# A two-layer encoder trunk on one core: an issue order fixed for the DMA queue, stores moved a few steps, and modulation sums divided differently between two stages

## The chip, the cores and the metric

The kernel runs on one core of a Trainium2 chip. A core has five engines that work side by side, each on its own list of instructions and strictly in that list's order: TensorE (PE, matrix products, with the loading of weights shown apart as PEld), VectorE (DVE), ScalarE (ACT), GpSimd (POOL) and SyncE (SP), which here does nothing but issue transfers (DMAs). They meet through semaphores. The metric is the time of one launch on the device, in microseconds (us); lower is better.

## What is computed

An encoder of two layers over 1024 tokens of width 1024, all in float32. Each layer has an attention half and a feed-forward half, and a vector `c` modulates both:

```
cond = silu(c)
mod = cond @ w_mod[l] + b_mod[l]                    # 1024 -> 6 * 1024
sh_a, sc_a, gt_a, sh_f, sc_f, gt_f = split(mod, 6)
h = rms_norm(x, g_attn) * (1 + sc_a) + sh_a
y = three attention groups over h @ w_in            # A: neighbourhood, B: window, C: dense
x = x + gt_a * (norms(y) @ w_o)
h = rms_norm(x, g_ffn) * (1 + sc_f) + sh_f
gate, up = split(h @ w_gu, 2)                       # 1024 -> 2 * 2816
x = x + gt_f * ((silu(gate) * up) @ w_down)         # 2816 -> 1024
```

A final RMSNorm closes the trunk. The modulation vector of a layer does not depend on the tokens, so its six groups of 1024 columns can be summed at any time before they are used: groups 0 to 2 before and in the attention half, 3 to 5 in the feed-forward half. In what follows "group (1, 2)" is layer 1, third group.

## The kernel before, in words

**Products.** Each float32 operand is split into a high and a low part (ACT casts, DVE or POOL subtracts), and each product is three matmuls. Gate/up and down are done by Strassen's scheme with Winograd's sums: a 2 x 2 block product in seven products instead of eight. In gate/up a step `q` (0 to 21) is one block of 256 columns of the gate matrix (even `q`) or of the up matrix (odd `q`). It has seven products of twelve matmuls; the first five steps have two of their seven done earlier, while the activations are still being normalised. Two steps make a pair, and there are eleven pairs in a layer.

**Gate/up.** `gu_raw` loads the weights of a step (two tiles `wr` of 512 KB), `a_parts` forms sums `ws` on DVE and splits them into tiles `wpt`, and the class `Ahead` keeps eight such parts ready in front of TensorE. `gu_product` runs a product and takes its result out of PSUM: ACT copies it or applies silu, DVE adds, POOL multiplies. The finished pair stands in two tiles `sg`, and the pair after next uses the same two tiles. `g_steps` lists what is left to do with a finished pair: three stores to the DRAM array `gpd` (blocks 11, 22, 21), four subtractions in place on DVE that make the Strassen sums out of the same tiles, and four stores of those sums (t1, t3, t2, t4). After each product `g_step` does one entry of the list, and many entries are empty.

**Down.** `w_first` loads blocks `w` of the down weights (256 KB each), `b_load` reads `gpd` back two units at a time into `graw`. `units()` splits both, and 77 units of twelve matmuls (`ps_d`) follow, the first eleven of which use block 11 of each pair.

**Modulation.** A group is summed over eight row blocks of `w_mod`: a load `wmt`, then on DVE a multiply-add into `acc` (`mod_add`), then `mod_flush`: two parts `acch` and `accl`, matmuls with a matrix of ones (`ps_mod`), and a short reduction. There are two ways in. `mod_next` does one row block of 1024 columns a call (512 KB). It is called after the last projections of the attention input: six times beside the values (`ps_v`) and beside each of the twelve half projections `ps_ab`, there once in layer 0 and three times in layer 1. It loads into four tiles shared with the tables `zt`. `mod_stream` does half a row block a step (512 columns, 256 KB) in gate/up, into the two tiles `sq`, at the products of even index from `q` = 2 on. Layer 0 finishes its own groups there and sums (1, 0) and (1, 1); layer 1 sums the other four beside `ps_ab`.

**What sets the order.** Python emits the instructions, and a scheduler then orders each engine's list by a modelled time. `pin([sp], True)` takes SP out of its hands: SP issues in the order in which Python emitted. It is pinned beside `ps_ab` and in down, and free in gate/up. DVE and ACT are free in all three. A transfer at the head of SP's list that has to wait for a tile holds up all that stand behind it.

Every operation is recorded at line 49 of the kernel (a wrapper around the engines), so the profile is read by tile names.

Of the kernel before, what the change touches and what calls it, by code (L numbers as in the profile page):

```python
# [23 lines left out]
H = 512  # L24
# [61 lines left out]
def trunk(ctx: ExitStack, tc, A, C, out):  # L86
    nc = tc.nc
    pe, act, dve, pool, sp = (
        Engine(tc, e) for e in (nc.tensor, nc.scalar, nc.vector, nc.gpsimd, nc.sync)
    )  # L90

    def pin(engines, on):
        for e in engines:
            e.pinned = on
# [123 lines left out]
    def sub(out, a, b, eng=dve):  # L218
        eng.tensor_tensor(out=out, in0=a, in1=b, op=ALU.subtract)
# [130 lines left out]
    def mod_next(psp, shared, l):  # L350


        if psp is not None:
            mod_flush(psp)
        if not todo or todo[0][0] > l or going["step"] == KC:
            return
        if going["step"] == 0:
            going["acc"] = cp.tile([P, 1024], F32, name="acc", tag="acc")
        mod_step(*todo[0], going["step"], going["acc"], shared)
        going["step"] += 1  # L360
        if going["step"] == KC:
            mod_parts(slice(0, shared[3]), shared)
# [128 lines left out]
    ps_cm, psl = open_pool("ps0", bufs=8, space=PSUM)  # L491
# [200 lines left out]
    for l in range(2):  # L692
# [200 lines left out]
        for t in range(10):  # L893
# [4 lines left out]
            elif t < 6:  # L898
                i = t + 4 if t < 2 else t + 2
# [8 lines left out]
            if 0 < t < 9:  # L908
                t1, t2 = qts.pop(t - 1)
# [26 lines left out]
        ab_cm, ab = open_pool("ab", side="left")  # L936
# [44 lines left out]
        for oc in range(NE, 8):  # L981
            w = wab
            for half in range(2):
                if half == 0 and oc < 7:
                    wab = split_tile(wst.pop(0), KC)
                ps = ab_proj(w, half)
                for _ in range(1 + 2 * l):
                    mod_next(psl, (ab, "zt", 4, 1024), l)
                if store:
                    store()  # L990
                if half == 0 and oc < 6:
                    wst.append(w_ab(l, oc + 2))
                store = ab_split(oc, half, ps, ab)
# [418 lines left out]
        pairs = {}  # L1412
# [3 lines left out]
        for n in range(-AHEAD - 1, N + 1):  # L1416
# [27 lines left out]
            for end, (chunks, width) in norms.items():  # L1444
                if begins[end] <= m <= end and (m - begins[end]) % 8 == 7:
                    i = (m - begins[end]) // 8
                    if end not in gss:
                        gss[end] = gss_tile()
                    for half in range(2):
                        what = lambda a=(chunks, gss[end], i, half): norm_sum(*a)  # L1450
# [25 lines left out]
        ps_cm, psl = open_pool("ps1", bufs=8, space=PSUM)  # L1476
        mp_cm, mp = open_pool("mp", side="left")
        NK = 6
        due = [("row", k) for k in (7, 0, 1)] + [("col", 6), ("col", 7)]
# [64 lines left out]
        nt_cm, ntp = open_pool("nt", side="left")  # L1544
# [85 lines left out]
        def x_tile(n, shape, name):  # L1630
            return xp.tile(shape, F32, name=name, tag=f"x{n}")
# [31 lines left out]
        def gu_product(q, p, a):  # L1663
            num, b, bank = p
            up = q % 2
            t = quads.setdefault(q, {})
            ps = product(num, t, bank, a, hb[b], 4)
            e, o = sg.get(q // 2, (None, None))
            lo, hi = slice(0, H), slice(H, S)

            def take(key, out=None):
                if out is None:
                    tag, bufs = ("u4", 1) if (q, num) == (4, 1) else ("u", 4)
                    out = ffp.tile([P, H], F32, name="u", tag=tag, bufs=bufs)
                t[key] = out
                act.copy(out, ps)

            def add(key):
                dve.tensor_tensor(out=t[key], in0=t[key], in1=ps, op=ALU.add)

            def done(dst, src, eng=dve):
                if up:
                    eng.tensor_tensor(out=dst, in0=dst, in1=src, op=ALU.mult)
                else:
                    act.activation(dst, src, AF.Silu)

            if num == 1:
                take("11")
            elif num == 2:
                add("11")  # L1690
                if e is not None:
                    done(e[:, lo], t["11"], pool)
            elif num == 6:
                take("12", None if up else e[:, hi])
            elif num == 5:
                take("22", None if up else o[:, hi])
            elif num == 7:
                take("x")
                t22 = t["22"]
                pool.tensor_tensor(out=t22, in0=t22, in1=t["x"], op=ALU.add)  # L1700
                done(o[:, hi], t["22"], pool)
            elif num == 3:
                add("12")
                done(e[:, hi], t["12"], pool)
            else:
                done(o[:, lo], ps)
                if up:
                    steps.extend(g_steps(q // 2, e, o))

        steps = []  # L1710

        def g_steps(b, e, o):


            b11, b12, b21, b22 = (t[:, i * H : (i + 1) * H] for t in (e, o) for i in range(2))

            def put(name, src):
                sp.dma_start(gpd[:, PLACE[name] + b, :], src)

            due = {  # L1720
                0: lambda: [put(*a) for a in (("11", b11), ("22", b22), ("21", b21))],
                6: lambda: sub(b11, b12, b11),
                7: lambda: (sub(b12, b22, b12), sub(b22, b22, b11), put("t1", b11)),
                8: lambda: (sub(b21, b21, b22), put("t3", b12), put("t2", b22)),
                9: lambda: put("t4", b21),
            }
            return [due.get(i, lambda: None) for i in range(10)]

        def g_step(n=1):
            for what in steps[:n]:  # L1730
                what()
            del steps[:n]

        def gu_start(b):
            sg[b] = [x_tile(4 + 2 * (b % 2) + i, [P, S], "sg") for i in range(2)]


# [35 lines left out]
            shifted_sub(b21, b21, shift(2 * i + 1), t2)  # L1773
            h_split("t4", i, b21, pool)

        mods_due = mod_stream(psl, (ntp, "sq", 2, H), (1, 2))
        bs = []
        rows = None
        norm = rstd_rows(ssq, ntp, psl)
# [1 line left out]
        for q in range(EARLY):  # L1781
            for i in range(2):
                a = [w[:, 4 * i : 4 * i + 4] for w in early[q]]
# [13 lines left out]
        for part in (t3_part, t4_part):  # L1797
            for q in range(1, 4):
                part(q, *bs[q])
        for q in range(NF):  # L1800
            if q % 2 == 0:
                gu_start(q // 2)
            if q < EARLY:
                up = q % 2
                e = sg[q // 2][0][:, 0:H]
                if up:
                    pool.tensor_tensor(out=e, in0=e, in1=quads[q]["11"], op=ALU.mult)
                else:
                    act.activation(e, quads[q]["11"], AF.Silu)
            for i, p in enumerate(PRODUCTS[2 if q < EARLY else 0 :]):  # L1810
                gu_product(q, p, ahead.get())
                ahead.fill()
                g_step()
                if i % 2 == 0 and q > 1:
                    next(mods_due, None)
        for _ in mods_due:
            pass
# [71 lines left out]
        due = {}  # L1889
# [33 lines left out]
            for i, u in enumerate(us):  # L1923
                at_unit(u, lambda n=n0 + 2 * i, half=half: x_back(n, half))

        pin([sp], True)
        for t in range(NB):
            w_first("11", t, wap)
            if t in (1, 3):
                b_load(t // 2)  # L1930
        ahead = Ahead(units())
        ahead.fill(4)
        g_step(len(steps))
        xt = blocks(xp)
        b_load(2)
        acc_a = [psl.tile([P, 512], F32, name="ps_d", tag="mm") for _ in range(4)]
# [195 lines left out]
```

## Time and profile before

| what | time |
|---|---|
| median of 3 runs | 2643.97 us (2643.47 to 2654.1) |
| the profiled execution | 2648.72 us, its span 2646.6 us |
| granted TensorE clock, mean | 0.967 |
| layer 0: `ps_ab` beside modulation | 193.2 to 263.5 us |
| layer 0: gate/up, down | 641.7 to 1110.7 us, then to 1334.9 us |
| layer 1: `ps_ab` beside modulation | 1479.3 to 1583.8 us |
| layer 1: gate/up, down | 1953.8 to 2402.7 us, then to 2628.0 us |

Rows of the profile name an instruction by output and input tile, with their shapes. In a view of waits, "A <- B: total, times, longest" says how long the instructions of A stood idle until B was done. In a view in order of time, a bracket at the end of a row holds the idle time in front of it and what ended it. In a view by stretches each engine has its busy time and its number of instructions, followed by the granted clock of TensorE, the busy share of the DMA engines and GB/s. "SPq" is SP issuing a transfer; a row of several transfers covers the time from the first to the last issue.

### The profile page before, as it was taken

What the parts mean: (1) busy time and instruction counts of PE and PEld (TensorE: products, weight loads), DVE (VectorE), ACT (ScalarE), POOL (GpSimd) and SP (SyncE); (2) the same over time, 40 slices, a digit from 0 to 9 for tenths busy, and PEclk for the clock granted to TensorE, in tenths of its full rate; (3) what the DMA queues carried; (4) which work ended last, traced back from release to release, by engine and by line L of the source; (5) the groups of instructions that cost most, each with busy time, mean ns of one, the idle gap of its engine ahead of it and who ended that gap; (6) DMA issues with size and microseconds to landing.
All of it is one profiled execution on the core that took longest, in us unless ns stands there. A gap on an engine that the chain in (4) does not pass through costs nothing.

```text
span 2646.6 us, 34697 instructions
## 1 busy us (share of the span) xinstructions
PE 2467.0 (93%) x12071; PEld 2037.8 (77%) x12071; DVE 1809.6 (68%) x2896; ACT 1241.2 (47%) x2335; POOL 964.5 (36%) x881
## 2 busy tenths in 40 slices
PE   5899999899799899899999789998998999998998
PEld 5677899777577788788877668997876888887887
DVE  6845999987965755376747568999677454454865
ACT  5421888934433333344523118888444333333443
POOL 5541445543643343300135104456445444340001
PEclk8999999999999999999999889999998999999999
DMA  8467205074343523396424662050623332327743
GB/s 260 141 186 231 64 21 160 19 247 147 119 142 109 163 81 107 109 278 183 138 82 120 212 209 57 21 155 21 207 80 119 116 104 92 108 84 231 218 140 107
DMA packets 288862, 356.48 MB, mean 135 GB/s; under 512 B 32824, under 2 KB 207120, under 8 KB 288688
## 3 DMA queue, kind: packets, MB, share of 16 engines
q1 hardware_dynamic: 288384, 354.13, 43.5%
q8 instruction: 95, 1.56, 0.2%
q14 instruction: 79, 0.65, 0.1%
q0 software_dynamic: 304, 0.14, 0.0%
HBM read 267.31 MB, written 87.85 MB: 134 GB/s over the span
## 4 chain that ended last, share of the span: by engine, by line
PE 50%; DVE 6%; issue 4%; DMA 2%; ACT 2%; POOL 1%; SPq 1%; POOLq 0%; DVEq 0%; ACTq 0%
PE ps_w L49 21%; PE ps_d L49 13%; PE ps_o L49 3%; PE pv L49 3%; PE ps_ab L49 2%; PE T L49 2%; PE ps_v L49 2%; PE sC L49 1%; DVE xb L49 1%; DVE acc L49 1%; PE ps_st L49 1%; SPq L49 1%; ACT pr L49 0%; DMA cst<-const_rope_dram 0%; PE sA L49 0%
## 5 line engine op out<-in xcount | busy, mean ns | idle before, releaser
L49 PE MATMUL ps_d<-wpt 128*128 128x512 f32 x1848 | 428.2, 393 | 18.0 <-ACT wpt L49 17.7
L49 PEld LDWEIGHTS ps_d<-wpt 128*128 128x128 f32 x1848 | 348.4, 189 | 93.4 <-ACT wpt L49 18.3
L49 POOL TENSOR_SCALAR pr<-pr,rs 128x1024 f32<-128x1024 f32 (+4 forms) x256 | 208.1, 815 | 223.7 <-DVE rs L49 209.4
L49 POOL TENSOR_TENSOR wlo<-wst,whi 128x1024 fp32r<-128x1024 f32 x58 | 146.8, 2534 | 290.0 <-ACT whi L49 281.6
L49 PE MATMUL pv<-pt,vs 128*128 128x256 f32 x1216 | 201.2, 297 | 11.7 <-DVE y L49 5.3
L49 DVE TENSOR_TENSOR pt<-T,pt 128x512 fp32r<-128x512 f32 x304 | 199.7, 681 | 10.2 <-ACT pt L49 8.6
L49 POOL TENSOR_TENSOR wpt<-ws,wpt 128x512 fp32r<-128x512 f32 x88 | 119.5, 1360 | 217.9 <-ACT wpt L49 133.4
L49 PE MATMUL T<-identr,pr 128*128 128x128 f32 x1320 | 192.1, 274 | 5.0 <-POOL pr L49 2.1
L49 ACT CAST pt<-T 128x512 fp32r<-128x512 f32 x304 | 170.1, 587 | 40.3 <-PE T L49 38.4
L49 PEld LDWEIGHTS pv<-pt,vs 128*128 128x128 f32 x1216 | 161.0, 190 | 26.1 <-DVE y L49 12.8
L49 ACT COPY u<-ps_w 128x512 f32<-128x512 f32 x132 | 77.4, 586 | 220.1 <-PE ps_w L49 220.0
L49 PEld LDWEIGHTS T<-identr,pr 128*128 128x128 f32 x1320 | 156.7, 141 | 27.3 <-POOL pr L49 4.4
L49 ACT CAST wpt<-w 128x512 fp32r<-128x512 f32 x154 | 95.5, 620 | 171.6 <-PE ps_d L49 155.5
L49 POOL TENSOR_TENSOR sg<-sg,u 128x512 f32<-128x512 f32 x88 | 124.6, 1416 | 138.2 <-ACT u L49 78.8
L49 DVE TENSOR_TENSOR wpt<-w,wpt 128x512 fp32r<-128x512 f32 x154 | 108.3, 703 | 77.7 <-ACT wpt L49 77.4
L49 DVE TENSOR_TENSOR wpt<-ws,wpt 128x512 fp32r<-128x512 f32 x88 | 78.5, 892 | 102.6 <-ACT wpt L49 102.5
L49 DVE TENSOR_TENSOR ws<-wr 128x512 f32<-128x512 f32 x88 | 86.3, 981 | 90.5 <-POOL wpt L49 81.0
L49 ACT CAST wpt<-ws 128x512 fp32r<-128x512 f32 x176 | 108.2, 622 | 78.7 <-PE ps_w L49 37.6
L49 PE MATMUL ps_w<-ht3h,wpt 128*128 128x512 f32 x352 | 116.6, 414 | 25.7 <-ACT sg L49 24.4
L49 DVE SCALAR_TENSOR_TENSOR acc<-wmt,condT,acc 128x1024 f32<-128x1024 f32 (+1 forms) x85 | 116.6, 1375 | 27.0 <-DMA wmt<-in_w_mod_dram 26.1
L49 ACT CAST whi<-wst 128x1024 fp32r<-128x1024 f32 x74 | 77.0, 1049 | 114.5 <-PE ps_o L49 38.6
L49 DVE TENSOR_TENSOR wpt<-graw,wpt 128x512 fp32r<-128x512 f32 x154 | 108.9, 707 | 28.6 <-ACT wpt L49 28.6
(258 smaller groups left out, 6301.6 us busy)
## 6 DMA issues: line engine op xcount, KB each, us to landing
wr<-in_w_gu_dram SPq DMA_DIRECT2D x92, 512.0 KB, 3.6
gpd<-sg SPq DMA_DIRECT2D x154, 256.0 KB, 2.1
graw<-gpd SPq DMA_DIRECT2D x76, 512.0 KB, 3.8
wmt<-in_w_mod_dram SPq DMA_DIRECT2D x63, 512.0 KB, 5.0
w<-in_w_down_dram SPq DMA_DIRECT2D x110, 256.0 KB, 5.4
qk<-qkd SPq DMA_DIRECT2D x44, 512.0 KB, 7.2
qkd<-qko SPq DMA_DIRECT2D x64, 256.0 KB, 3.9
wst<-in_w_o_dram SPq DMA_DIRECT2D x32, 512.0 KB, 4.5
```

The lines of the kernel that those rows point to most:

```text
L49: ins = op(*args, **kwargs)
```

## The change

1. Layer 1 calls `mod_next` once, not three times, beside each `ps_ab` half.
2. In gate/up `mod_stream` runs to group (1, 4), not (1, 2), and takes a step at every product instead of every second one.
3. The list of a pair has 13 entries, not 10. The first three stores move from entry 0 to 3, the subtractions from 6, 7, 8 to 8, 9, 10, and the stores of the sums to entries 9, 11 and 12.
4. The lists are kept per pair. `gu_start` first finishes every pair but the latest.
5. SP is pinned from the start of the loop over `q`, not from the start of down. The last pair's stores, which the free order had put among the first loads of down, are now emitted behind the first loads of down.

```diff
-                for _ in range(1 + 2 * l):
-                    mod_next(psl, (ab, "zt", 4, 1024), l)
+                mod_next(psl, (ab, "zt", 4, 1024), l)
...
-                    steps.extend(g_steps(q // 2, e, o))
+                    steps.append(g_steps(q // 2, e, o))
...
             due = {
-                0: lambda: [put(*a) for a in (("11", b11), ("22", b22), ("21", b21))],
-                6: lambda: sub(b11, b12, b11),
-                7: lambda: (sub(b12, b22, b12), sub(b22, b22, b11), put("t1", b11)),
-                8: lambda: (sub(b21, b21, b22), put("t3", b12), put("t2", b22)),
-                9: lambda: put("t4", b21),
+                3: lambda: [put(*a) for a in (("11", b11), ("22", b22), ("21", b21))],
+                8: lambda: sub(b11, b12, b11),
+                9: lambda: (sub(b12, b22, b12), sub(b22, b22, b11), put("t1", b11)),
+                10: lambda: sub(b21, b21, b22),
+                11: lambda: (put("t3", b12), put("t2", b22)),
+                12: lambda: put("t4", b21),
             }
-            return [due.get(i, lambda: None) for i in range(10)]
-
-        def g_step(n=1):
-            for what in steps[:n]:
-                what()
-            del steps[:n]
+            return [due.get(i, lambda: None) for i in range(13)]
+
+        def g_step():
+            if steps:
+                steps[0].pop(0)()
+                if not steps[0]:
+                    steps.pop(0)
+
+        def g_finish(pairs):
+
+            while len(steps) > pairs:
+                g_step()
 
         def gu_start(b):
+            g_finish(1)
...
-        mods_due = mod_stream(psl, (ntp, "sq", 2, H), (1, 2))
+        mods_due = mod_stream(psl, (ntp, "sq", 2, H), (1, 4))
...
+        pin([sp], True)
         for q in range(NF):
...
                 g_step()
-                if i % 2 == 0 and q > 1:
+                if q > 1:
                     next(mods_due, None)
...
-        pin([sp], True)
         for t in range(NB):
             w_first("11", t, wap)
...
         ahead.fill(4)
-        g_step(len(steps))
+        g_finish(0)
```

## The prediction, made before the change was run

> **What bounds the kernel now.** I read the page's totals and chain first, then the same stages of the two layers side by side, since the change makes a stage of one layer like that of the other, then the waits inside them.
>
> ```profile
> span 2646.6 us, 34697 instructions
> ...
> PE 50%; DVE 6%; issue 4%; DMA 2%; ACT 2%; POOL 1%; SPq 1%; POOLq 0%; DVEq 0%; ACTq 0%
> ```
>
> The chain runs over TensorE, so time is won only where TensorE stands idle or runs at a low granted clock. The next rows are stretches: `ps_ab` in layers 0 and 1, gate/up in 0 and 1, the first 22 us of down in 0 and 1, and gate/up without modulation. The columns are PE, PEld, DVE, ACT, POOL (busy, instructions), clock, DMA share, GB/s.
>
> ```profile
> 193.20:263.50 70.30, 69.00 (x297) 55.69 (x296) 38.31 (x43) 11.04 (x16) 13.90 (x5) 1.00 0.73 221
> 1479.30:1583.80 104.50, 81.85 (x305) 62.88 (x304) 72.45 (x73) 11.02 (x16) 13.53 (x5) 0.85 0.70 227
> 641.70:1110.70 469.00, 442.40 (x1853) 354.70 (x1853) 284.97 (x350) 170.00 (x298) 200.28 (x140) 0.97 0.34 110
> 1953.80:2402.70 448.90, 435.63 (x1841) 351.07 (x1841) 240.41 (x288) 170.19 (x298) 195.87 (x140) 0.98 0.29 95
> 1110.70:1133.00 22.30, 12.93 (x50) 10.16 (x49) 8.72 (x15) 5.78 (x11) 0.00 (x0) 0.85 1.01 302
> 2402.70:2424.00 21.30, 13.69 (x50) 10.94 (x50) 9.07 (x15) 6.11 (x11) 0.00 (x0) 0.76 1.01 306
> ...
> 1007.00:1048.00 41.00, 41.00 (x178) 33.26 (x177) 19.16 (x24) 15.84 (x28) 16.69 (x13) 1.00 0.29 97
> ```
>
> Three excesses stand out. The same projections take 70.3 us in layer 0 and 104.5 us in layer 1. Gate/up takes 469.0 us in layer 0, which has modulation in it, and 448.9 us in layer 1, which has none. At the start of down TensorE is busy for 13 of 22 us in both layers.
>
> **Step 1: `ps_ab` in layer 1, -34.2 us.** First the waits of TensorE there, layer 1 and then layer 0 (total, times, longest), then the DVE work that reads `wmt` in the two stretches.
>
> ```profile
> PE ps_mod L49 <- DVE acch L49: 22.5, 4, 9.0
> ...
> PE ps_mod L49 <- DVE acch L49: 1.3, 1, 1.3
> ...
> 193.20:263.50 70.30, 22.27 (x17) 1.00 0.73 221
> 1479.30:1583.80 104.50, 45.19 (x32) 0.85 0.70 227
> ```
>
> Layer 1 adds 32 row blocks (45.2 us of DVE) there, and TensorE, which takes `ps_mod` in its own order, stands four times behind the end of a group. The change removes 16 of the 32 loads (8 MB) and adds and two of the four flushes. What is left is, in the instruction order of the changed program, what layer 0 has now: the same DVE list from the first `qko` to the last, less two adds with which layer 0 begins a third group. So 70.3 us replaces 104.5. The gain cannot be much more. At least the idle time goes, 22.5 - 1.3 = 21.2 us; the rest of the 34.2 is matmuls at a granted clock of 0.85, which go back to 1.00 with the idle time. I take 34.2 and keep 21 as the other end.
>
> **Step 2: gate/up of layer 0, -12.5 us.** The 16 blocks come back as 32 half blocks, 66 in all instead of 34, beside products. Matmuls first: layer 0 has 1853 - 1841 = 12 more than layer 1, six flushes of two; the change makes it ten flushes, 20 matmuls. At 41.00 / 178 = 0.23 us that is 4.6 us, so the stage cannot fall below 448.9 + 4.6 = 453.5. Today's other excess is 469.0 - 448.9 - 2.8 = 17.3 us of waits, and this chain shows the largest of them:
>
> ```profile
> PE ps_w L49 <- ACT sg L49: 21.6, 4, 8.1
> ...
> 907.21 0.62 PE L49 MATMUL ps_w<-h11h,wpt 128*128 128x512 f32 x2
> ...
> 917.98 1.64 SPq L49 DMA_DIRECT2D gpd<-sg  x3
> ...
> 921.62 0.69 DVE L49 TENSOR_TENSOR sg<-sg 128x512 f32<-128x512 f32 x1 [1.14 <-DMA gpd<-sg]
> 922.22 0.68 DVE L49 TENSOR_TENSOR u<-u,ps_w 128x512 f32<-128x512 f32 x1
> ...
> 922.94 0.63 ACT L49 ACTIVATE sg<-u 128x512 f32<-128x512 f32 x1 [9.29 <-DVE u L49]
> ...
> 924.10 1.22 PE L49 MATMUL ps_w<-ht3h,wpt 128*128 128x512 f32 x2 [5.58 <-ACT sg L49]
> ```
>
> Read from below: the fifth product of a gate step waits for ACT, ACT for a DVE add, the add stands behind a subtraction in place, and that one waits for the store of the block it overwrites, which SP issued 10.8 us after the step began, behind modulation loads. In steps of 12 x 0.23 = 2.8 us the fifth product is due 11.2 us after the first, and the add started at 15.0 us to make it 5.6 late. So an add up to about 9.4 us after the step's begin costs nothing. In layer 1, without modulation, it comes earlier:
>
> ```profile
> 2129.24 0.62 PE L49 MATMUL ps_w<-h11h,wpt 128*128 128x512 f32 x2
> ...
> 2132.54 1.65 SPq L49 DMA_DIRECT2D gpd<-sg  x3
> ...
> 2136.67 0.68 DVE L49 TENSOR_TENSOR u<-u,ps_w 128x512 f32<-128x512 f32 x1
> ...
> wr<-in_w_gu_dram SPq DMA_DIRECT2D x92, 512.0 KB, 3.6
> gpd<-sg SPq DMA_DIRECT2D x154, 256.0 KB, 2.1
> ```
>
> With SP pinned and the stores at entry 3, SP issues both `wr` loads of a step (1 MB) and then the three stores; the modulation loads come one a product instead of in bursts. The first `wr` lands 3.6 us after its issue; at the 300 GB/s that the start of down shows, the second needs 1.7 us more and the three stores 0.9 each, so the last store lands near 8 us, and the add starts near 8.7: inside 9.4, by little. Hence I leave 3 us of the 17.3: 453.5 + 3 = 456.5, -12.5. Queued behind SP's waits are only loads due seven products (19 us) later, since `Ahead` and the second raw tile cover them. DVE has room: 19.16 of 41 us without modulation. The extra adds cost this:
>
> ```profile
> L49 DVE SCALAR_TENSOR_TENSOR acc<-wmt,condT,acc x14: 739/750/1840, 881.3 to 911.2; 128x512 f32<-128x512 f32 x14
> ...
> DMA wmt<-in_w_mod_dram: 12.1, 8
> ```
>
> At 0.75 us, 32 of them are 24 us over some 13 steps (250 us, one step of `mod_stream` a product); at 1.84 us, 59 us; and the group shown made DVE wait 12.1 us for its loads. All of it fits into DVE's idle time, but each late microsecond in front of that add counts. Bounds: 453.5 (-15.5), and every group paying double, 453.5 + 2 x 17.3 = 488 (+19).
>
> [...]
>
> **Step 3: the start of down, -12.4 us.**
>
> ```profile
> 1109.09 1.30 SPq L49 DMA_DIRECT2D w<-in_w_down_dram  x2
> ...
> 1112.28 0.68 DVE L49 TENSOR_TENSOR sg<-sg,ps_w 128x512 f32<-128x512 f32 x1
> ...
> 1118.45 12.77 PE L49 MATMUL ps_d<-wpt 128*128 128x512 f32 x48 [7.63 <-ACT wpt L49]
> ...
> 1122.86 2.54 SPq L49 DMA_DIRECT2D gpd<-sg  x4
> 1125.49 1.41 SPq L49 DMA_DIRECT2D graw<-gpd  x1
> ...
> 1132.96 4.37 PE L49 MATMUL ps_d<-wpt 128*128 128x512 f32 x18 [1.75 <-ACT wpt L49]
> ...
> 2410.48 16.72 PE L49 MATMUL ps_d<-wpt 128*128 128x512 f32 x62 [7.61 <-ACT wpt L49]
> ```
>
> Let T be the end of gate/up, 1110.7 us in layer 0. The first `w` goes out at T - 1.6, held behind the last pair's stores, and TensorE starts at T + 7.7. In the new order eleven `w` and two `graw` stand in front of those stores and wait only for the activations' tiles, free five products (14 us) before T. Then what is late next is DVE: its list has the last product's multiply (T + 1.6) in front of the first split, so the two splits (0.7 us each) let TensorE start near T + 2 to 3; I take 2. The first four units last 4 x 2.8 = 11.2 us, to T + 13.2. The fifth needs the third `graw`, now behind all seven last stores. Their subtractions stand behind the split of the fifth `w`, which waits for a buffer of unit 0 (T + 4.8); with 1.3 us for the split and 2.4 for four subtractions the stores go out near T + 8.5 and `graw` at T + 9. Today it takes 7.5 us from that issue to the matmul, with the queue full; with it empty 3.6 for 512 KB and 1.3 for the split, some 5. I take the middle, T + 15.4, against T + 22.3 in layer 0 and T + 20.9 in layer 1 (48 of the 50 matmuls of its row): -6.9 and -5.5. Bounds: no wait at all, T + 13.2 (-16.8 in both together), and T + 20 (-3.2).
>
> **Step 4: gate/up of layer 1, +1 us.** The same SP order without modulation; the add at 8.7 us instead of 7.4. Bounds 0 and nine pairs at 1 us, +9. The calls of `g_finish(1)` move two or three stores in the early pairs and cost nothing, as the pair's tiles are due a product or more later; if that cover is gone, it shows as a wait for ACT `sg` at step 4.
>
> **Sum.** -34.2 - 12.5 - 12.4 + 1 = -58.1. The profiled execution took 2648.7 us, 4.8 over the median of the runs, so 2590.6 for it and 2586 for the median. The ends of the four steps give -66 and -7; I let the likeliest range from 2574 to 2606.
>
> **Rivals.** (a) *The adds cost in gate/up what they saved.* Step 2 at its bad end, +19: for it speaks that DVE waited 12.1 us in one group and that the add has under 1 us to spare; against it that the loads are spread over twice the products. -34.2 + 19 - 12.4 + 1 = -27, 2617. (b) *Down starts no earlier in effect:* the fifth unit is late by as much as the first four are early, as its data still pass SP behind eleven loads. For it speaks the DMA share of 1.01. 2586 + 12 = 2598. (c) *Slower:* the three stores behind the `wr` loads make the add late in every steady pair of both layers, nine a layer, at the 5.6 us shown. Then gate/up is at 453.5 + 50 = 504 and 448.9 + 50 = 499, and the sum -34.2 + 34.7 + 50 - 12.4 = +38, 2682. It decides from 4.2 us a pair on (-34.2 - 15.5 - 12.4 + 18 x 4.2 = +13). The spare time of 0.7 us speaks for it, but the stores would have to land 5 us later than now computed. (d) *The pin does nothing* for steps 2 and 3, the scheduler's order being as good: step 1 alone, 2610.
>
> **How the numbers follow.** The forecast has 0.57, (a) 0.16, (b) 0.13, (c) 0.06, (d) 0.08. Half a per cent, 13 us, is about what a measurement can tell from no change. All but (c) and the tail of (a) are faster by more: 0.88; within, 0.06; slower, 0.06. The range reaches from 2572, below the best end, to (a), 2618.
>
> **What would show it.** Step 1: `ps_ab` of layer 1 in 70 to 72 us, clock 1.00, DMA `wmt` of 512 KB down by 16. Step 2: gate/up of layer 0 at 456 us, no wait for ACT `sg` beyond the first steps; wrong, if such waits stand in most gate steps. Step 3: the first `ps_d` within 3 us of the last `ps_w`, one wait of about 2 us before the fifth unit; wrong, if that wait is 8. Step 4: 449 to 451 us. The forecast falls if the two layers' gate/up both grow.

## The result, and the profile after

The changed kernel takes 2606.9 us (median of 4 runs, 2604.13 to 2610.04), the kernel before 2643.72 us beside it: a ratio of 0.9852, 95% interval 0.9825 to 0.9879. The forecast was 2586 with a range of 2572 to 2618. So the direction and the range held, and the gain was 37 us where 58 were forecast. The profiled execution took 2610.04 us, 38.7 less than that of before.

From the page of the changed kernel, the span and the chain that ended last:

```profile
span 2608.3 us, 34639 instructions
...
PE 47%; DVE 7%; issue 4%; DMA 3%; ACT 2%; POOL 2%; SPq 1%; POOLq 0%; DVEq 0%; ACTq 0%
```

TensorE still carries the chain, with a smaller share than before (50%); DVE, DMA and POOL each have a point more. The next rows are stretches of the changed kernel, with the columns of the prediction's first table: `ps_ab` of layer 1, gate/up of layers 0 and 1 from the `ps_st` that close the normalisation to the last `ps_w`, and the first 23.9 us of down in both layers.

```profile
1477.40:1547.70 70.30, 69.04 (x298) 55.71 (x297) 37.76 (x43) 11.03 (x16) 14.05 (x5) 1.00 0.72 213
641.60:1108.50 466.90, 444.74 (x1868) 354.82 (x1868) 341.30 (x400) 170.01 (x299) 208.50 (x140) 0.98 0.40 131
1915.60:2362.30 446.70, 437.30 (x1848) 350.69 (x1848) 246.08 (x287) 171.08 (x299) 197.01 (x140) 0.98 0.30 98
1108.50:1132.40 23.90, 15.49 (x58) 11.99 (x59) 13.04 (x21) 8.21 (x15) 0.00 (x0) 0.81 0.96 290
2362.30:2386.20 23.90, 15.73 (x54) 12.13 (x55) 11.81 (x19) 7.78 (x15) 0.00 (x0) 0.79 0.94 282
```

`ps_ab` came out at the forecast's 70.3 us. Gate/up of layer 0 came only to 466.9 us; with the same two marks the kernel before has 470.8 (640.0 to 1110.8), since the prediction's 469.0 leaves out the first 1.8 us. Layer 1 has 446.7 against 450.8. In front of the first mark of layer 0, and so outside these times, `ps_st` waits 8.7 us for `ssq`, 2.3 us more than before. Down's first stretch still has TensorE busy for 15 to 16 of 24 us at a clock of 0.8.

The waits of TensorE in gate/up of layer 0 (total, times, longest) show what took the place of the old ones:

```profile
PE ps_w L49 <- ACT sg L49: 8.4, 2, 8.1
PE ps_mod L49 <- DVE accl L49: 7.2, 4, 3.4
PE ps_mod L49 <- DVE acch L49: 3.7, 4, 1.9
```

Three of the four old waits for `sg` (21.6 us together) are gone. What is left is the 8.1 us early in the stage, which both kernels have, and one of 0.3 us. New are eight waits of `ps_mod`, 10.9 us.

The start of down in layer 0, in order of time; the gate/up stage ends at T = 1108.45:

```profile
1102.66 1.26 SPq L49 DMA_DIRECT2D w<-in_w_down_dram  x2
...
1106.60 7.82 SPq L49 DMA_DIRECT2D w<-in_w_down_dram  x7
...
1109.73 11.45 PE L49 MATMUL ps_d<-wpt 128*128 128x512 f32 x48 [1.28 <-ACT wpt L49]
...
1114.52 8.64 SPq L49 DMA_DIRECT2D gpd<-sg  x7
...
1119.94 2.87 DVE L49 TENSOR_TENSOR sg<-sg 128x512 f32<-128x512 f32 x4 [3.97 <-DMA gpd<-sg]
...
1123.25 0.40 SPq L49 DMA_DIRECT2D graw<-gpd  x1
...
1127.69 0.62 ACT L49 CAST wpt<-graw 128x512 fp32r<-128x512 f32 x1 [12.69 <-DMA graw<-gpd]
...
1128.36 31.98 PE L49 MATMUL ps_d<-wpt 128*128 128x512 f32 x129 [7.18 <-ACT wpt L49]
```

TensorE starts 1.3 us after T, as forecast, does four units and then stands for 7.18 us in front of the fifth, whose `graw` SP issued only at T + 14.8, behind the seven stores. From T to the end of down's matmuls layer 0 takes 224.1 us (223.9 before), layer 1 228.3 (225.0 before).

The balance of the two profiled executions: `ps_ab` -34.3, gate/up of layer 0 -3.9, gate/up of layer 1 -4.1, down +0.2 and +3.3, everything else together +0.5 (the 2.3 us in front of gate/up are in it); the sum, -38.3, is the difference of the two spans.

### The profile page after: what moved, and what is told of

It reads as the page before. It is cut to its first block, busy times and chain, and to the rows that moved or that the text cites. A ratio compares the mean times of both kernels' runs of the same rounds, so it can differ in the third digit from the quotient of the medians.

```text
span 2608.3 us, 34639 instructions
## 1 busy us (share of the span) xinstructions
PE 2455.3 (94%) x12071; PEld 2024.9 (78%) x12071; DVE 1836.1 (70%) x2916; ACT 1241.4 (48%) x2335; POOL 974.2 (37%) x881
## 4 chain that ended last, share of the span: by engine, by line
PE 47%; DVE 7%; issue 4%; DMA 3%; ACT 2%; POOL 2%; SPq 1%; POOLq 0%; DVEq 0%; ACTq 0%
PE ps_w L49 19%; PE ps_d L49 12%; PE ps_o L49 3%; PE pv L49 3%; PE ps_ab L49 2%; PE T L49 2%; PE ps_v L49 2%; PE sC L49 2%; DMA wmt<-in_w_mod_dram 1%; SPq L49 1%; DVE wpt L49 1%; DVE acc L49 1%; DVE xb L49 1%; DVE sg L49 1%; DVE ws L49 1%
## 5 line engine op out<-in xcount | busy, mean ns | idle before, releaser
L49 PE MATMUL ps_d<-wpt 128*128 128x512 f32 x1848 | 432.1, 395 | 17.7 <-ACT wpt L49 17.3
L49 PEld LDWEIGHTS pv<-pt,vs 128*128 128x128 f32 x1216 | 160.6, 189 | 25.4 <-DVE y L49 12.5
L49 DVE SCALAR_TENSOR_TENSOR acc<-wmt,condT,acc 128x512 f32<-128x512 f32 (+1 forms) x99 | 125.1, 1273 | 46.9 <-DMA wmt<-in_w_mod_dram 46.4
L49 DVE TENSOR_REDUCE rs<-sC 128x1 f32<-128x1024 f32 x96 | 116.9, 1220 | 10.2 <-PE sC L49 9.9
```

Source lines behind the costliest of these rows:

```text
L49: ins = op(*args, **kwargs)
```

## The experiments

In each group of runs the kernel before was timed on the same chip, with medians from 2644 to 2653 us from group to group. Kernels are therefore compared by their ratio to it. "Gate/up" is the time between the two marks above, "down" that from the last `ps_w` (T) to the end of its matmuls (layer 0 / layer 1), both from the profiled execution; "next wait in down" is the longest wait behind the first `ps_d`, up to the seventh unit.

| kernel | us | ratio (95%) | gate/up 0 | waits: sg / ps_mod | gate/up 1 | first `ps_d` after T | next wait in down | down |
|---|---|---|---|---|---|---|---|---|
| before | 2643.7 | 1 | 470.8 | 21.6 / 0 | 450.8 | 7.6 / 7.6 | 1.8 / 0 | 223.9 / 225.0 |
| after | 2606.9 | 0.9852 (0.9825-0.9879) | 466.9 | 8.4 / 10.9 | 446.7 | 1.3 / 1.8 | 7.2 / 6.4 | 224.1 / 228.3 |
| e1 modulation alone | 2623.2 | 0.9898 (0.9869-0.9928) | 482.4 | 26.5 / 1.2 | 450.2 | 7.5 / 7.7 | 1.4 / 0 | 224.4 / 225.3 |
| e2 order alone | 2620.9 | 0.9894 (0.9869-0.9919) | 448.7 | 6.5 / 0 | 445.1 | 1.8 / 1.7 | 7.6 / 6.6 | 224.7 / 226.6 |
| e3 third graw first | 2600.6 | 0.9817 (0.9793-0.9842) | 465.8 | 6.6 / 10.1 | 445.1 | 0.6 / 2.3 | 4.9 / 4.8 | 221.9 / 225.1 |
| e4 flush later | 2597.0 | 0.9802 (0.9776-0.9829) | 456.8 | 9.8 / 0.3 | 443.7 | 2.0 / 2.1 | 7.0 / 6.3 | 224.3 / 226.8 |
| e5 both | 2596.7 | 0.9804 (0.9788-0.9820) | 459.1 | 10.7 / 0.4 | 446.7 | 1.8 / 1.7 | 6.0 / 4.8 | 223.3 / 224.0 |
| e6 stores first | 2614.0 | 0.9869 (0.9846-0.9891) | 466.2 | 6.5 / 8.6 | 444.9 | 13.4 / 13.3 | 0 / 0 | 228.4 / 230.8 |
| e7 w12 later | 2602.9 | 0.9833 (0.9815-0.9852) | 466.6 | 6.5 / 10.9 | 443.7 | 2.1 / 2.5 | 6.3 / 7.7 | 224.0 / 227.7 |
| e8 spread | 2576.8 | 0.9736 (0.9718-0.9754) | 456.5 | 9.4 / 0.3 | 446.7 | 1.9 / 1.7 | 0 / 0 | 214.9 / 218.7 |
| e9 old entries | 2614.9 | 0.9857 (0.9833-0.9882) | 470.9 | 13.4 / 7.0 | 445.1 | 10.4 / 10.0 | 0.7 / 0 | 226.0 / 227.5 |
| e10 pin from down | 2628.1 | 0.9910 (0.9882-0.9937) | 481.9 | 24.5 / 1.2 | 451.7 | 1.3 / 1.4 | 7.3 / 6.6 | 223.2 / 226.3 |
| e11 spread, w12 early | 2577.8 | 0.9744 (0.9724-0.9764) | 457.3 | 10.7 / 0.3 | 445.1 | 1.9 / 2.0 | 0 / 0 | 216.1 / 219.0 |

The theories at the outset: step 3 failed because the third `graw` stands in SP's queue behind work that is not urgent (rival: the transfer rate is used up, whatever the order); step 2 fell short because the parts of a modulation sum come one product, not two, ahead of their matmuls (rival: DVE is simply late with so many adds); and the waits for `sg` went because SP is pinned (rivals: because modulation loads are spread evenly, or because the stores come later).

### e1: the modulation alone

The kernel before, with

```diff
-                for _ in range(1 + 2 * l):
-                    mod_next(psl, (ab, "zt", 4, 1024), l)
+                mod_next(psl, (ab, "zt", 4, 1024), l)
...
-        mods_due = mod_stream(psl, (ntp, "sq", 2, H), (1, 2))
+        mods_due = mod_stream(psl, (ntp, "sq", 2, H), (1, 4))
...
-                if i % 2 == 0 and q > 1:
+                if q > 1:
```

> The kernel before with the division of the modulation alone (one row block a half projection beside ps_ab in layer 1, one step of mod_stream a product up to group (1, 4)); SP's order, the stores and the start of down stay as they were. ps_ab of layer 1 should take 70.3 us by every theory. Gate/up of layer 0 decides. If the fixed order of SP and the later stores are what took the waits for ACT sg away, these waits stay here and new ones for ps_mod join them: gate/up of layer 0 near 477 us (469.0 plus 1.8 for eight more matmuls plus 7 to 11 of ps_mod waits, less what falls together), the whole near 2644 - 34 + 8 = 2618. If the spreading of the loads over single products took them away, gate/up of layer 0 is near the 465 us of the changed kernel and the whole near 2606 to 2610. Down starts as before, TensorE about 7.7 us after the last ps_w.

Measured: `ps_ab` of layer 1 at 70.3 us, gate/up of layer 0 at 482.4 us. Its waits:

```profile
PE ps_w L49 <- ACT sg L49: 26.5, 6, 8.1
```

The waits for `sg` stay and grow from four to six. The modulation alone is worth -34.3 beside `ps_ab` and +11.6 in gate/up; the even spreading of its loads took no wait away. The 7 to 11 us of `ps_mod` waits that were expected to join did not come: they are 1.2 us.

### e2: the order alone

The changed kernel, with the three lines of e1 put back as they were.

> The changed kernel with the old division of the modulation: SP's fixed order, the stores three entries later and down's first loads in front of the last stores, and nothing else. ps_ab of layer 1 should be back at 104.5 us. If the order took the waits for ACT sg away, gate/up of layer 0 comes to 448.9 + 2.8 + 1 to 4 = 453 to 456 us and no ps_mod wait is over 1 us, since a step of the stream at every second product leaves 5.6 us between the parts and their matmuls; layer 1's gate/up 447 as in the changed kernel, down +3, so 2644 - 14 - 4 + 3 = 2629. If the order does nothing for layer 0 and the even spreading did it, gate/up of layer 0 stays near 469 and the whole is near 2643.

Measured: gate/up 448.7 us in layer 0, 22 us less than before, and 445.1 in layer 1; `ps_ab` of layer 1 is back at 104.8. Its waits in gate/up of layer 0:

```profile
PE ps_w L49 <- ACT sg L49: 6.5, 1, 6.5
```

Only the one at the start is left. The order is therefore worth 22 us in gate/up of layer 0, more than the 13 to 16 expected, and 5.7 in layer 1. It gains nothing in down. With the order, the added modulation costs gate/up 466.9 - 448.7 = 18 us, of which 10.9 are the waits of `ps_mod`; without it, in e1, it costs 11.6. So the two halves of the change do not add: traced, e1 saves 21.1 us and e2 26.4, and both together 38.3. The waits of `ps_mod` stand only where the new order and the new division meet (0 in e2, 1.2 in e1).

### e10 and e9: which half of the order

e10 is the changed kernel with the later entries, but SP pinned only from down on; e9 has SP pinned in gate/up, but the entries of before.

```diff
-        pin([sp], True)
         for q in range(NF):
...
+        pin([sp], True)
         for t in range(NB):
             w_first("11", t, wap)
```

> The changed kernel with the later entries kept, but SP free in gate/up and pinned only from the loads of down on, as it was before. If the fixed order took the waits for ACT sg away, they come back here: gate/up of layer 0 near 480 us, layer 1 near 450, the whole 2607 + 14 + 4 = 2625. If the later entries did it, gate/up stays at 465 to 468 and 444 to 447 us and the whole near 2607.

```diff
-                3: lambda: [put(*a) for a in (("11", b11), ("22", b22), ("21", b21))],
-                8: lambda: sub(b11, b12, b11),
...
+                0: lambda: [put(*a) for a in (("11", b11), ("22", b22), ("21", b21))],
+                6: lambda: sub(b11, b12, b11),
...
-            return [due.get(i, lambda: None) for i in range(13)]
+            return [due.get(i, lambda: None) for i in range(10)]
```

> The changed kernel with SP pinned in gate/up, but with the list of a pair as it was before: stores at entry 0, subtractions at 6, 7 and 8, stores of the sums at 7, 8 and 9. It tells which half of the new order took the waits for ACT sg away. If the fixed order alone did it, gate/up stays at 466 to 467 us in layer 0 and 444 to 447 in layer 1, the whole at 2604 to 2610. If the later entries are needed as well, the stores at entry 0 hold the wr and modulation loads behind them until the pair's last product is multiplied, or the subtractions come in front of adds of the next gate step: gate/up of layer 0 at 472 us or more with waits for ACT sg or wpt in most pairs, the whole 2612 or more.

Measured, first for e10 and then for e9, the waits in gate/up of layer 0:

```profile
PE ps_w L49 <- ACT sg L49: 24.5, 6, 6.6
```

```profile
PE ps_w L49 <- ACT sg L49: 13.4, 3, 8.1
PE ps_mod L49 <- DVE accl L49: 4.2, 4, 1.5
```

Without the pin there are six waits, as in e1, and gate/up (481.9 and 451.7 us) is near that of e1 (482.4 and 450.2). So the later entries alone do next to nothing, and the pin did most of it. With the pin, the later entries take away about 5 us more of `sg` waits in layer 0 (13.4 to 8.4) and nothing in layer 1; e9's 470.9 us lie between what its two theories had given. The entries matter at another place, too: with the stores at entry 0, the last pair's first three stand in front of down's loads again, and TensorE starts down at T + 10. e9's profiled execution, with a span of 2606.9 us, was the fastest of its runs; the ratio, 0.9857, doesn't separate it from the changed kernel.

### e4: the flush one step later

```diff
-        going["wait"] = width < 1024
+        going["wait"] = 2 if width < 1024 else 0
...
-            going["wait"] = False
+            going["wait"] -= 1
```

> The changed kernel with one more step of mod_stream between the two parts acch and accl and the matmuls that take them (two skipped steps instead of one). If gate/up of layer 0 lost its time because a step is now one product and not two, so that TensorE reaches ps_mod 2.8 us after the parts were listed instead of 5.6, the eight waits for acch and accl (10.9 us together) fall below 2 us and gate/up of layer 0 comes from 465.2 to about 456, the whole to 2607 - 9 = 2598. If DVE is late there anyway (slow adds, loads that land late), the lateness shows at the next products as waits for ACT sg or wpt, gate/up stays at 462 to 466 and the whole at 2604 to 2607.

First the changed kernel around one flush, DVE and TensorE in order of time:

```profile
730.90 0.69 DVE L49 TENSOR_TENSOR sg<-sg 128x512 f32<-128x512 f32 x1 [3.84 <-DMA gpd<-sg]
...
733.32 1.41 DVE L49 TENSOR_TENSOR sg<-sg 128x512 f32<-128x512 f32 x2
734.65 1.52 DVE L49 CAST acch<-acc 128x512 fp32r<-128x512 f32 x1
736.09 0.68 DVE L49 TENSOR_TENSOR acc<-ps_mod,identr 128x512 f32<-128x512 f32 x1
...
736.22 0.50 PE L49 MATMUL ps_mod<-acch,onesr 128*128 128x512 f32 x1 [0.30 <-DVE acch L49]
...
736.69 1.75 DVE L49 TENSOR_TENSOR wpt<-ws,wpt 128x512 fp32r<-128x512 f32 x1
738.36 0.67 DVE L49 TENSOR_REDUCE sums<-acc 128x4 f32<-128x512 f32 x1
738.96 1.15 DVE L49 TENSOR_TENSOR accl<-acc,acch 128x512 fp32r<-128x512 f32 x1
...
740.16 0.50 PE L49 MATMUL ps_mod<-accl,onesr 128*128 128x512 f32 x1 [3.45 <-DVE accl L49]
```

The matmuls of a group's first half ran at 729.7 and never wait. The second half's stand 6.3 us later in TensorE's list. In between DVE waits 3.84 us for a store, and then has the pair's four subtractions, a split of weights and the reduction of the first half, and only then `accl`. In the three other groups that are late DVE has no pause there; its list is full. In the kernel before the two halves are 8.6 us apart (746.9 and 755.5) and no `ps_mod` waits.

Measured with the extra step: the halves are 8.6 to 9.0 us apart, and in gate/up of layer 0

```profile
PE ps_w L49 <- ACT sg L49: 9.8, 2, 8.1
...
PE ps_mod L49 <- DVE accl L49: 0.3, 1, 0.3
```

Gate/up falls to 456.8 us, 14.0 less than before, the ratio from 0.9852 to 0.9802. The adds are as many, and DVE waits for its loads as before; had DVE been late in general, the time would have stayed. In e1 and e10, with 5.8 us between the halves and SP free, `ps_mod` waits for 1.2 us only: in e10's first group DVE has `acch` next after the first half's matmuls (738.0 after 737.5). So the short distance costs only beside the pin: the changed kernel differs from e10 in the pin alone and has 10.9 us. That this works through DVE's list, which has other work or a wait in between, is read from these traces and not tried by itself.

### e3: the third graw in front of the stores

```diff
-        g_finish(0)
-        xt = blocks(xp)
         b_load(2)
+        g_finish(0)
+        xt = blocks(xp)
```

> The changed kernel with one line moved: the load of the third graw is emitted in front of the last pair's seven stores instead of behind them. If the place in SP's queue is what makes the fifth unit of down late, the third graw goes out near T + 6.5 instead of T + 14.8 (T is the last ps_w of gate/up), and the wait of 7.2 us in layer 0 and 6.4 us in layer 1 before the fifth unit falls to 0 to 2: 2607 - 10 to 13.6 = 2593 to 2597. If it is late because the eleven w loads fill the DMA engines, whatever the order, the wait stays above 4 us and the whole near 2604 to 2607. If the time comes back later (the last stores and the subtractions in place behind them then hold DVE), the waits move to units 6 to 14 and the whole stays near 2607 as well.

Measured, the start of down in layer 0:

```profile
1113.91 0.71 SPq L49 DMA_DIRECT2D graw<-gpd  x1
1114.71 11.53 SPq L49 DMA_DIRECT2D gpd<-sg  x7
...
1126.96 0.56 SPq L49 DMA_DIRECT2D graw<-gpd  x1
...
1131.93 28.34 PE L49 MATMUL ps_d<-wpt 128*128 128x512 f32 x114 [4.89 <-ACT wpt L49]
```

The third `graw` goes out at T + 5.3 and the wait before the fifth unit is gone, but two units later TensorE stands for 4.89 us: the fourth `graw` is now the one behind the stores. The wait was not removed, it moved by two units and lost 2.3 us (1.6 in layer 1). Since the eleven `w` stand in front of the third `graw` here as well, and it is in time, their bytes alone are not what made it late. The ratio is 0.9817, 0.35% below the changed kernel's, with intervals that overlap.

### e5: e3 and e4 together

> The changed kernel with the flush one step later and the third graw in front of the last seven stores. The two edits act in different stages. If they are independent, their gains add: 2597.0 - 6.3 = 2591, with gate/up of layer 0 near 457 us, and in down one wait of about 5 us before the seventh unit (the fourth graw, still behind the stores), none of 6 to 7 us before the fifth. If the loads of down's start only share a fixed transfer rate, the third graw buys nothing on a second try and the time stays near 2597.

The ratio of 0.9804 is that of e4 alone (0.9802). Against e4 the traced waits at the start of down fall by 1.0 and 1.5 us only, which is below what the runs resolve. The gains did not add as expected; what e3 gave in its own group may in part be the scatter between groups.

### e7: fewer bytes at the start of down

```diff
-            at_unit(t, lambda t=t: w_first("12", t, wbp))
+            at_unit(5 + t, lambda t=t: w_first("12", t, wbp))
```

> The changed kernel with down's loads of the blocks w12 issued five units later (they are used eleven units after their present issue), all else in place. If the waits at the start of down come from too many bytes for the transfer rate (the DMA share is 1.01 there), 1.25 MB less in the first 14 us takes 4 us away per layer: 2607 - 8 = 2599. If they come from the place of the third graw in SP's queue, ahead of which no w12 stands, the wait before the fifth unit stays at 6 to 7 us and the time at 2604 to 2608.

The waits before the fifth unit stay: 6.3 us in layer 0, 7.7 in layer 1. But SP issues all `w12` behind the third `graw`, so the run says only that what follows it does not hold it up; on the loads ahead of it, and so on the transfer rate, it decides nothing. The ratio, 0.9833, is 0.2% below the changed kernel's, too little to be read.

### e6: the last stores in front again

```diff
+        g_finish(0)
         for t in range(NB):
             w_first("11", t, wap)
...
-        g_finish(0)
         xt = blocks(xp)
```

> The changed kernel with the last pair's seven stores back in front of all loads of down, SP still pinned: undoes the last part of the change alone. If putting down's loads in front of the stores won nothing, because what TensorE gains at its start it loses before the fifth unit, then TensorE starts 7 to 9 us after T, no later wait is over 2 us, and the time is within 3 us of 2607. If the part does win what the forecast gave to it (6 us a layer), this kernel is at 2607 + 12 = 2619. If the stores in front delay more than the free order did, since a pinned SP stands still until the subtractions in place are done, TensorE starts near T + 12 and the time is 2612 to 2620.

SP and TensorE in order of time, T = 1109.06:

```profile
1088.68 25.69 SPq L49 DMA_DIRECT2D gpd<-sg  x11
...
1114.47 1.29 SPq L49 DMA_DIRECT2D w<-in_w_down_dram  x2
...
1122.48 37.77 PE L49 MATMUL ps_d<-wpt 128*128 128x512 f32 x155 [13.42 <-ACT wpt L49]
```

A pinned SP stands in front of the last stores until the pair's last blocks and their subtractions are done, and TensorE starts at T + 13.4, with no later wait. Down takes 4.3 and 2.5 us more than in the changed kernel. So putting the loads in front does win something against pinned stores, but nothing against the order of before, in which the scheduler had mixed the two (T + 7.6).

### e8 and e11: only what is due next

e8 has the later flush, and at the start of down six `w`, three `graw`, and then in each unit what is due soon:

```diff
-        for t in range(NB):
+        for t in range(6):
             w_first("11", t, wap)
...
-        g_finish(0)
-        xt = blocks(xp)
         b_load(2)
...
                 b_load((u + 6) // 2)
+            for tw in range(6 + 2 * u, min(8 + 2 * u, NB)):
+                w_first("11", tw, wap)
+            if u < 6:
+                g_step()
+                g_step()
+            if u == 5:
+                g_finish(0)
+                xt = blocks(xp)
```

and `w12` five units later as in e7, and the first four reads of `xb` at units 6, 6, 7 and 8.

> Built from the above: the flush one step later; at the start of down only six w, three graw ahead, then in each of the first units two more w, the next graw, and two entries of the last pair's list in place of all seven stores at once; w12 five units later, the first four xb reads at units 6 to 8. If each wait at the start of down is a graw behind work in SP's queue that is not urgent, no wait over 2 us is left after the first unit in either layer, the time is 2597 - 7 - 6 = 2584, and down takes 217 us in layer 0 against 224. If the transfer rate is the limit, waits of 4 us and more show up at later units (8 to 12) and the time is 2590 to 2597. If the later w12 or xb come too late, waits stand at units 10 to 16.

Measured: 2576.8 us, ratio 0.9736 (0.9718 to 0.9754), 1.2% below the changed kernel. Layer 0, SP and TensorE from the start of down, T = 1094.47:

```profile
1092.60 1.58 SPq L49 DMA_DIRECT2D w<-in_w_down_dram  x2
...
1096.37 28.92 PE L49 MATMUL ps_d<-wpt 128*128 128x512 f32 x125 [1.91 <-ACT wpt L49]
...
1098.28 3.37 SPq L49 DMA_DIRECT2D graw<-gpd  x2
...
1101.70 2.67 SPq L49 DMA_DIRECT2D w<-in_w_down_dram  x4
...
1104.46 1.57 SPq L49 DMA_DIRECT2D gpd<-sg  x3
```

After the first wait of 1.91 us TensorE runs through. Down takes 214.9 and 218.7 us, 9.2 and 9.6 less than in the changed kernel, and less than the 217 expected for layer 0. Against e4, which has the later flush alone, the ratio falls by 0.7%. The edits at the start of down came together, so which of them are needed is not shown, but for `w12`, which e11 takes out.

e11 is e8 with the `w12` loads where the changed kernel has them:

```diff
-            at_unit(5 + t, lambda t=t: w_first("12", t, wbp))
+            at_unit(t, lambda t=t: w_first("12", t, wbp))
```

> The kernel with the spread start of down, but with the w12 loads back at units 0 to 10, where the changed kernel has them. If the order in SP's queue alone decides, the graw loads still stand in front of what each unit does not need yet, no wait over 2 us appears after the first unit, and the time stays within 5 us of 2577. If the transfer rate sets in once the order is right, 1.25 MB more in the first 14 us (4 us at 300 GB/s) brings waits of 3 to 5 us back at units 4 to 8 of both layers, with the half clock behind them, and the time is 2585 to 2592.

Measured: ratio 0.9744 (0.9724 to 0.9764), no wait over 0.3 us in the units after the start. The first 14 us of down in layer 0, first in the changed kernel and then in e11:

```profile
1108.45:1122.45 14.00, 11.45 (x48) 8.86 (x48) 8.63 (x14) 4.37 (x8) 0.00 (x0) 1.00 0.94 277
```

```profile
1097.10:1111.10 14.00, 12.12 (x53) 9.71 (x53) 9.47 (x15) 7.76 (x15) 0.00 (x0) 1.00 1.01 297
```

The DMA engines are busier in e11 (1.01 against 0.94), and the waits are gone: the place in SP's queue was the cause, and the transfer rate alone was not.

## Why the prediction was right, and where it was not

**Step 1, right.** Forecast 104.5 to 70.3 us at a clock of 1.00; measured 70.3 at 1.00. e1 shows the same with nothing else changed.

**Step 2, short by 8.6 us: two errors of opposite sign.** The waits for `sg` went as reasoned, and e10 shows that they stay without the pin. But the step's -12.5 is -14.3 for the order (17.3 us of waits down to 3) and +1.8 for the modulation (20 matmuls in place of 12), and the runs have -22.1 (e2) and +18.2 (from e2 to the changed kernel). The order won 7.8 us more: the step took layer 1 as its floor, which had a wait to lose itself, and e2 lies 4.8 us below the floor for its six flushes (446.9 by the prediction's marks, against 448.9 + 2.8). The modulation cost 16.4 more, and the mis-sized term is the flush. The step counted "ten flushes" as 20 matmuls, 4.6 us, and left out that a step of `mod_stream` that is taken at every product shortens the distance between a sum's parts and the matmuls that read them. Together with the pin that cost 10.9 us of `ps_mod` waits, and e4, which gives the distance back, comes to 14.0 us less than before, where 12.5 were forecast. The extra adds were a smaller matter; the groups of before and after, by form, the columns being busy time and mean ns, then the idle time in front:

```profile
L49 DVE SCALAR_TENSOR_TENSOR acc<-wmt,condT,acc 128x512 f32<-128x512 f32 x30 | 30.6, 1027 | 21.1 <-DMA wmt<-in_w_mod_dram 21.1
```

```profile
L49 DVE SCALAR_TENSOR_TENSOR acc<-wmt,condT,acc 128x512 f32<-128x512 f32 x58 | 61.8, 1083 | 40.5 <-DMA wmt<-in_w_mod_dram 40.5
```

An add takes 1.08 us on average after, 1.03 before; the long value of 1.84 us, at which the step put its upper figure for the added ones, 59 us, lies far above that mean. In the trace of the changed kernel the 23 of 58 adds during which POOL is idle take 0.74 to 0.75 us, the 35 others 1.31 us on average, and every add of more than 0.76 us is one of these. Why an add beside POOL's work can take longer is not shown. The 40.5 us in which DVE waits for `wmt` cost nothing by themselves, for e4 has 38 us of them in a stage that is 10.1 us shorter.

**Step 3, wrong.** Forecast -12.4 us, measured +3.5 (0.2 and 3.3). TensorE's start, T + 2, was right (T + 1.3 and T + 1.8). The term that failed is "the stores go out near T + 8.5 and `graw` at T + 9": they went out from T + 6.1 to T + 14.7, and `graw` at T + 14.8 (layer 1: T + 14.3). It failed in three places. The activations' tiles were taken to be free at T - 14; the first `w` went out at T - 5.8 in both layers, just when the third-last product ends (its last matmul starts at 1102.47, `w` at 1102.66). The step gave no time to the issue of eleven `w`, of which the last seven took 7.8 us. And it let the subtractions wait for DVE's own list alone: they stood 3.97 us until the first of the stores had landed, 5.4 us after it went out at 1114.52, and the last four stores could only follow them. So the fifth unit started at T + 19.9 and T + 21.3, where T + 15.4 was forecast (T + 15.25 by the step's own figures) and the kernel before has T + 22.1 and T + 21.0. This is rival (b): the fifth unit is late by about as much as the first four are early. Its stated reason, the DMA share of 1.01, is not enough, as e3 and e11 show; but where the median store of the kernel before lands after 2.1 us, the load of the DMA engines, a share of 0.97 over those 5.4 us, may be part of them; that is an estimate from these figures and was not tried.

The step also left out that the clock was lower behind the long pauses here, 0.50 over the first 5 us. These are stretches of 5 us behind a wait in down of the changed kernel; the waits in front of them were 1.28, 7.18, 1.77 and 6.40 us:

```profile
1109.80:1114.80 5.00, 5.00 (x21) 3.84 (x22) 3.73 (x7) 3.42 (x7) 0.00 (x0) 1.00 1.14 319
1128.40:1133.40 5.00, 5.00 (x12) 3.89 (x13) 4.30 (x7) 3.12 (x6) 0.00 (x0) 0.50 1.02 322
2364.10:2369.10 5.00, 5.00 (x14) 3.68 (x15) 4.34 (x7) 3.55 (x7) 0.00 (x0) 0.67 1.15 316
2383.60:2388.60 5.00, 5.00 (x12) 3.89 (x13) 4.24 (x7) 3.09 (x6) 0.00 (x0) 0.50 0.66 201
```

Behind the waits of 7.18 and 6.40 us 12 matmuls take the time of 21 to 24, which is some 2.5 us beside the wait itself. From the fifth unit to the end of down the changed kernel takes 204.2 and 207.0 us, the kernel before 201.8 and 204.0; with the starts above that gives the +0.2 and +3.3. The kernel before has its slow stretch once in each layer, too, at its first unit (0.66 and 0.50). The changed one has it at the fifth unit instead, and in layer 1 also in part at the first (0.67), where (1 - 0.67) x 5 = 1.6 of the 3.3 us that layer 1 lost went.

**Step 4, of the wrong sign.** Forecast +1, measured -4.1: a wait of 3.8 us for `sg` early in the stage went with the pin, too (10.4 us in two waits before, 6.6 in one after; e10, without the pin, has 10.3). The step looked only at when the add comes in a steady pair. Kernels with the same pinned code in this stage lie between 443.7 and 446.7 us, so the size is good to some 3 us.

**The rivals.** (a) did not happen as written, for gate/up of layer 0 did not grow; but beside the new order the added modulation takes back 18 us there of the 34 that it saves beside `ps_ab`, and only the order's 22 us hide it. (b) happened. (c) is excluded: in the changed kernel no wait for `sg` is over 0.4 us but the one early in the stage. (d) is excluded: the order alone takes 22 us off gate/up of layer 0.

**What was luck.** The whole, 2606.9 us, lies nearer to (d)'s 2610 than to the forecast, although (d) is false: what the order wins in gate/up is spent by the flush and in down. The range held since the misses (8.6 us in step 2, 15.9 in step 3, 5.1 the other way in step 4) partly cancel. The bad ends of the four steps, -21 + 19 - 3 + 9, give +4 and not -7; the range did not use that sum.

## What to carry to other kernels

An issue order pinned by hand puts every transfer behind all that stands in front of it (in e6 the first `w` of down behind eleven stores whose issue took 25.7 us), so for each reader one must ask what its load stands behind, how long that takes to issue and what it waits for; here moving a block of stores past a block of loads only moved the wait, from 7.6 us before the first unit to 7.2 and 6.4 before the fifth, while issuing each unit's own needs just ahead of it (e8) left 1.9 and 1.7 at the first unit and none behind it. When a background stream is advanced twice as often, a distance that is counted in its steps shrinks in time (here from 8.6 us to about 6); look for the matmul that reads its result, not only for the cost of its work. And a long wait of TensorE was dearer than its length, here by 1.5 to 3 us behind waits from 4.8 us on (an estimate from the clock of 0.50 to 0.70 in the stretches behind them), while most of the measured waits up to 2.3 us left it at 1.00.

## What the runs showed of the hardware

The granted clock after a pause at the start of down has three looks. Behind waits of 4.8 to 13.4 us the first 5 us run at 0.50 to 0.70: 0.53 behind 4.89 us in e3, 0.50 behind 7.18 us in the changed kernel, 0.66 behind 7.63 us in layer 0 of the kernel before. The next two are the stretches behind the 13.42 us of e6 and behind 7.30 us in layer 0 of e10:

```profile
1122.50:1127.50 5.00, 5.00 (x12) 3.89 (x13) 4.35 (x7) 3.14 (x6) 0.00 (x0) 0.50 1.17 313
```

```profile
1144.20:1149.20 5.00, 5.00 (x16) 4.01 (x17) 4.25 (x7) 3.64 (x7) 0.00 (x0) 0.70 0.91 275
```

The length of the wait alone does not set the value: 7.18 us in the changed kernel were followed by 0.50, 7.30 us in e10 by 0.70. Behind 0.6 to 2.3 us the clock is mostly 1.00 (0.60 and 2.25 us in e3, 1.28 in the changed kernel, 1.91 in e8), but 0.67 and 0.68 behind 1.77 us in the changed kernel and 1.74 us in e8, both in layer 1, while 1.7 us in layer 1 of e2 left 1.00. Cut finer, the 0.67 is first a clock of 1.00 and then one of 0.50:

```profile
2364.10:2365.70 1.60, 1.60 (x6) 1.02 (x7) 1.60 (x3) 1.48 (x3) 0.00 (x0) 1.00 1.04 362
2365.80:2369.10 3.30, 3.30 (x9) 2.56 (x9) 2.64 (x5) 2.07 (x4) 0.00 (x0) 0.50 1.21 293
```

If the slow part of every such stretch runs at the 0.50 of these rows, a mean of 0.70 over 5 us is 3.0 us of it, and 0.50 over 5 us with 0.89 over the next 5 (layer 1 of the changed kernel) is 6.1: an estimate of 3.0 to 6.1 us for the slow stretch here. What starts one 1.7 us after the end of so short a pause stays open, as does why the clock is lower behind a pause at all.

In the changed kernel the seven `w` behind the first four took 1.1 us each to issue on average, the first four 0.6. What slows SP there was not tried.
